# Re-dealing the rows of a block inverse, moving three small steps, and joining two matmuls in a hybrid decoder layer

## The chip, the cores and the metric

One core of a Trainium2 chip runs the whole layer. The time is the device time of that core in microseconds; lower is better. The kernel before has a median of 1421.55 us over three runs (1421.29 to 1422.97).

## What is computed

The layer takes 256 tokens of width 2048, puts 16 learned meta tokens ahead of them (272 in all), and computes:

- an embedding LayerNorm and one input projection `p = h @ w_in`;
- **an RWKV-7 mixer** of 16 heads of 64. Per token, with state S, `S = S*decay + (S @ -kk) (kk*a)^T + v k^T` and `y = S r`, where `kk` is the key scaled by `k_k` and divided by its norm over the head;
- a causal stick-breaking attention of 16 heads of 64, in 128-query blocks;
- a head norm of both, an output projection, `h = LN(alpha*h + mix)`;
- **a gated MLP**: `gate, val = split(h @ w_up)`, a causal width-3 convolution on gate, `(silu(gate)*val) @ w_down`, and a last LayerNorm. w_up has 2 x 5632 columns.

All data is float32.

## The kernel before

**Precision.** Every float32 operand x of a matmul is split in two fp32r parts, hi = round(x) and lo = x - hi, and a product is three matmuls: hi*hi, hi*lo, lo*hi (`passes`, lines 225 to 229). Weights arrive in 512 KB pieces on SP's queue; ScalarE makes hi (L183), VectorE makes lo (L186). `weight(i)` issues these some pieces ahead.

**Stages.** (1) 0 to 65 us: embedding norm, the first projections, and `lora()`, which makes decay and in-context rate (`sg`) of all eight head pairs by small matmuls, each evicted by a sigmoid on ScalarE. (2) 65 to 566 us: the mixers. (3) 566 to 700 us: the output projection's end and the first LayerNorm. (4) 700 to 1150 us: the up projection, tile by tile: tile 2f is gate, 2f+1 is val; a gate tile's matmuls have 258 moving columns, a val tile's 256, and each accumulates 16 k tiles x 3 matmuls in one PSUM bank. `act` (L1067) then does the convolution, silu, product, and split. Four of the banks rotate. (5) 1150 to 1405 us: the down projection, with 512 moving columns and, in its last fifth, partly 256.

**The order of the mixer stage.** PE's order is written out by hand. The input projection's matmuls run through `weave`, which counts them; after each 16 a `slot()` lets waiting tasks issue their own PE work. A task is a generator that yields (slots to wait, rank, PSUM banks needed of the two `misc` banks). The order of the other engines is left to a scheduler that goes by program order and readiness; weight casts are put 8 places later (`LATER`). Per head pair j there are:

- `rwkv_front(j)` (L558): a scan `cum` of the log decay, its exponentials `Pt` and `Pinv`, then `sq`, the squared scaled key, in hi and lo parts; two slots later PE sums it by head (tile `ss`, L536 and L537), and the normalised key and the products BK follow;
- `rwkv_back(j)` (L605): the products AG; two slots later PE makes the block products `gram` (L622), 18 pairs of 64x64; VectorE masks them (L624) and multiplies BK by PC (L626). GpSimd's queue carries the strictly lower 32x32 blocks through DRAM (`dl`) into LT. One slot later comes `bonus`, two slots later `bkt`, transposes of BK and v;
- for odd j `inverse(q)` (L664), q = j // 2: it inverts 36 blocks of 32x32 on GpSimd by 31 steps of a multiply and an add. Y holds 108 partitions = 3 groups (RG) of rows x 36 blocks, each partition 11 rows (NR) of 32. Row r lies in group r // 11, slot r % 11, and step s works on `min(s + 1, 11)` slots x 31 - s columns. Y goes through DRAM (`dy`) into TT by four DMAs on GpSimd's queue, one for each of four groups of 32 partitions;
- `chain(q)` (L683): 18 slots (INVERSE) after the two backs are done, nine chunks of three small products, the second of which (L705) reads TT. They end in `y` (L735), which takes both misc banks.

SP carries only weights and a few small loads; GpSimd's queue carries dl, LT, dy, TT and Y's start value.

Of the kernel before, what the change touches and what calls it, by code (L numbers as in the profile page):

```python
# [15 lines left out]
P = 128  # L16
# [63 lines left out]
def constants():  # L80
    c = np.zeros((P, NCV), np.float32)

    def put(name, a):
        o, w = CV[name]
        c[: a.shape[0], o:o + w] = a

    i = np.arange(P)
    put("ident", np.eye(P))
    put("bd", (i[:, None] // 64 == i[None] // 64) / 32)
    put("ones", np.ones((P, P)))  # L90
    put("tri", i[:, None] >= i[None])
    s, t, kind = i[:, None] % CH, i[None, :2 * CH] % CH, i[None, :2 * CH] // CH
    put("maskg", np.where(kind == 0, s < t, s <= t))
    put("cen", np.eye(P) - (i[:, None] // 64 == i[None] // 64) / 64)
    m = np.full((P, SBW), NEG, np.float32)
    for n, (k0, c0, c1, q0) in enumerate(ZB):
        key, q = k0 + i[:, None], q0 + np.arange(c1 - c0)[None]
        ok = key < q
        if n == 2:
            ok &= key >= 256  # L100
        m[:, c0:c1][ok] = 0
    put("sbmask", m)
    r = np.ones((P, TP))
    r[:, ::CH] = 0
    put("reset", r)
    y0 = np.zeros((RG, NB, NR, CH))
    for n in range(CH):
        y0[n // NR, :, n % NR, n] = 1
    put("y0", y0.reshape(RG * NB, NR * CH))
    return c  # L110

# [2 lines left out]
def hybrid_layer(ctx, tc, xin, cst, pvec, w2a2, g2, ln2, w_in, w_out, w_up, w_down, out, dbg=None):  # L114
# [169 lines left out]
    with ExitStack() as es:  # L284
# [106 lines left out]
        def lora():  # L391
            for m in range(3):
                shift(acc[m], 24 + m, lw[m], Q0 if m else 0)
            S.activation(lw[0][:64], lw[0][:64], AF.Tanh)
            sh = [tp_.tile([P, T], F32R, tag="tmp", bufs=2, name=f"sh{n}") for n in range(2)]
            for n, (h, o) in enumerate(zip(half, half[::-1])):
                S.copy(sh[n][h], lw[0][h])
                V.tensor_sub(sl[n][h], lw[0][h], sh[n][h].bitcast(F32))
                S.copy(sh[n][o], lw[0][h])
            yield  # L400
            for m in (1, 2):
                S.activation(lw[m][:, Q0:], lw[m][:, Q0:], AF.Sigmoid)
            S.copy(g1h, lw[1][:, Q0:])
            V.tensor_sub(g1l, lw[1][:, Q0:], g1h.bitcast(F32))
            S.copy(g2s[:96], lw[2][:96, Q0:])
            V.tensor_sub(g2s[32:64], lw[2][32:64, Q0:], g2s[32:64].bitcast(F32))
            for j in range(NPAIR):
                t = mtile(F32, f"sg{j}")
                G.memset(t[:, :, :PAD], 0.0)
                for n, name in enumerate(("w0", "a0")):  # L410
                    ps = pst.tile([P, 512], F32, tag="tr", bufs=4, name=f"lora{j}{n}")
                    w = w2a2_r[:, n, j * P:j * P + P]
                    mm(ps[:, :T], lhsT=w, rhs=sh[n], start=True, stop=False)
                    mm(ps[:, :T], lhsT=w, rhs=sl[n], start=False, stop=True)
# [142 lines left out]

    def rwkv_front(j, st):  # L558

        assert j == 0 or "bv" in state[j - 1]  # L560
        a = sg[j][:, 1]
        cum = atile("cum", [P, TP])
        V.tensor_tensor_scan(out=cum, data0=reset, data1=sg[j][:, 0], initial=0.0, op0=ALU.mult, op1=ALU.add)
        S.activation(Pt[:, :, 1:], ch(cum), AF.Exp, scale=-DECAY)
        Pinv = cum
        S.activation(Pinv, cum, AF.Exp, scale=DECAY)
        sq = atile("sq", [P, TP])
        S.activation(sq, k_, AF.Square, scale=par("k_k", j))
        sq = halves(sq, "rn", "ss")
        yield 2, FULL, 1  # L570
        ps = misc("ss")
        by_head(ps[:, :TP], *sq)
        ss = atile("ss", [P, TP])
        V.tensor_scalar(out=ss, in0=ps[:, :TP], scalar1=16.0, scalar2=0.5e-24, op0=ALU.mult, op1=ALU.max)
        rn = atile("rn", [P, TP])
        S.activation(rn, ss, AF.Ln, scale=2.0 * KSC)
        S.activation(rn, rn, AF.Exp, scale=-0.5, bias=lnb[:, 1:2])
        y2 = atile("sq", [P, TP])
        S.activation(y2, rn, AF.Square)
        V.tensor_mul(ss, ss, y2)  # L580
# [12 lines left out]
        st["kkn"] = kkn
# [11 lines left out]
    def rwkv_back(j, st):  # L605
# [8 lines left out]
        rk = halves(rk, "rkh", "rkl", NQ)  # L614
        PC = st["PC"] = atile("PC", [P, NCH], bufs=4)
        S.copy(PC, Pt[:, :, CH])
        yield 2, SQUARE, 2
        for c0, n in parts:
            ps = misc("gram").rearrange("p (c n) -> p c n", n=2 * CH)
            for c in range(n):  # L620
# [18 lines left out]
            bonus[j // 2] = wide(f"bv{j // 2}")  # L639
        bv = st["bv"] = bonus[j // 2][:, j % 2, :NQ]  # L640
        V.scalar_tensor_tensor(bv, ps[:, :NQ], 32.0, v_[:, TP - NQ:], op0=ALU.mult, op1=ALU.mult)
        yield 2, FULL, 2
        R = st["R"] = [wide(f"R{j}{x}").rearrange("p n t -> p (n t)").rearrange("p (c f) -> p c f", c=NCH) for x in range(2)]
        for x in range(2):
            V.memset(R[x], 0.0)
# [18 lines left out]
    def inverse(q, LT, Y):  # L664
# [1 line left out]
        tmp = atile("ytmp", [P, NR, CH])  # L666
        n_ = RG * NB
        for s in range(CH - 1):
            n = min(s + 1, NR)
            m = CH - 1 - s  # L670
            G.tensor_tensor(out=tmp[:n_, :n, :m], in0=Y[:n_, :n, s:s + 1].to_broadcast([n_, n, m]),  # L671
                            in1=LT[:n_, s:s + 1, s + 1:].to_broadcast([n_, n, m]), op=ALU.mult)
# [1 line left out]
        nc.gpsimd.dma_start(dy.rearrange("b (g r) t -> g b (r t)", g=RG), Y[:n_].rearrange("p r t -> p (r t)"))  # L674
        for n in range(4):
            x, o = n % 2, n * CH
            nc.gpsimd.dma_start(TT[q % 2][o:o + CH, :, CH - x * CH:2 * CH - x * CH],
                                dy[n * NCH:n * NCH + NCH, :CH].rearrange("c r t -> r c t"))

    def first_of_all():  # L680
        return tc.high_priority(offset=AHEAD)
# [255 lines left out]
    h1stack = ctx.enter_context(ExitStack())  # L937
    h1p = pool(h1stack, "h1p", side="right")

    h1hi = h1p.tile([P, KT, NQ + 2], F32R, name="h1hi")  # L940
    h1lo = h1p.tile([P, KT, NQ + 2], F32R, name="h1lo")
    for n, name in enumerate(("ln1_g", "ln1_b")):
        S.copy(h1hi[:, :, NQ + n], pars(name))
        V.tensor_sub(h1lo[:, :, NQ + n], pars(name), h1hi[:, :, NQ + n].bitcast(F32))
# [119 lines left out]
        S.copy(ahi[:, f], t)  # L1064
        V.tensor_sub(alo[:, f], t, ahi[:, f].bitcast(F32))

    def act(f, pg, pval):  # L1067
        t = up.tile([P, SEQ], F32, tag="t", bufs=2, name=f"t{f}")
        gate(f, t, pg, pval)
        split(f, t)  # L1070

# [46 lines left out]
    for f in range(4, NF):  # L1118
        pair = []
        for m in range(2):  # L1120
            ps = bank(f"u{2 * f + m}")
            n = NQ if m == 0 else SEQ
            for hf in range(2):
                hi, lo = weight(wi)
                wi += 1
                for kk in range(8):
                    kt = hf * 8 + kk
                    passes(ps[:, :n], hi, lo, kk, *rhs(m, kt), kt == 0, kt == KT - 1)
            pair.append(ps)
        act(f, *pair)  # L1130
    ustack.close()
    h1stack.close()

# [134 lines left out]
```

## Time and profile before

| | us |
|---|---|
| median of three runs | 1421.55 |
| the profiled execution | 1419.27 |
| its span, first to last instruction | 1417.5 |
| granted TensorE clock, mean (1 is 2.4 GHz) | 0.974 |

A group of instructions is given by source line, engine and tile; a wait by who waited for whom. PE is the matmul stream, PEld its weight loads, DVE VectorE, ACT ScalarE, POOL GpSimd. Matmuls overlap in the records, so a matmul's own duration is longer than the step from one to the next.

### The profile page before, as it was taken

How to read it: one execution, taken by the hardware profiler on the slowest of the kernel's cores; microseconds unless marked ns; L12 is line 12 of the kernel's file. 1: busy time of each engine (PE TensorE's matmuls, PEld its weight loads, DVE VectorE, ACT ScalarE, POOL GpSimd, SP SyncE). 2: the span in 40 equal slices, each digit the busy share in tenths (PEclk: the TensorE clock that was granted, in tenths of full speed). 3: DMA queues.
4: the chain of work that ended last, by engine and by line, in shares of the span. 5: the costliest groups of instructions: out<-in, count | busy, mean ns of one | idle time of the engine just before them, and what ended most of it. 6: DMA issues, size and time to landing. Idle time of an engine off the chain costs nothing.

```text
span 1417.5 us, 26265 instructions
## 1 busy us (share of the span) xinstructions
PE 1336.2 (94%) x10540; PEld 1250.2 (88%) x10540; DVE 937.4 (66%) x1502; ACT 723.3 (51%) x1227; POOL 278.1 (20%) x417
## 2 busy tenths in 40 slices
PE   8988798799999999988999999999999999999996
PEld 5888687788889889988999999999999998888895
DVE  7678666889876878888755555555555554445445
ACT  6755555566656766445644444444444443333331
POOL 4107873047282000553100000000000000000002
PEclk8999999999999999999999999999999999999998
DMA  7444433344444335543556665665666566656662
GB/s 228 136 126 144 127 114 91 95 126 120 136 120 116 110 93 165 160 151 112 162 193 194 185 185 179 183 187 181 180 186 185 180 222 210 192 184 190 201 183 89
DMA packets 67642, 224.02 MB, mean 158 GB/s; under 512 B 9144, under 2 KB 10868, under 8 KB 67376
## 3 DMA queue, kind: packets, MB, share of 16 engines
q1 hardware_dynamic: 63392, 215.03, 49.0%
q0 software_dynamic: 3264, 4.18, 1.3%
q10 hardware_dynamic: 864, 3.15, 0.6%
q8 instruction: 82, 1.34, 0.4%
q14 instruction: 40, 0.33, 0.1%
HBM read 219.01 MB, written 3.30 MB: 157 GB/s over the span
## 4 chain that ended last, share of the span: by engine, by line
PE 69%; DVE 8%; POOL 3%; ACT 3%; issue 2%; DMA 2%; POOLq 0%; DVEq 0%; ACTq 0%
PE u L229 11%; PE u L227 11%; PE u L228 11%; PE d L1148 6%; PE d L1147 6%; PE d L1149 6%; DVE wlo L186 2%; PE S L481 2%; PE S L483 2%; PE S L479 2%; POOL ytmp L671 1%; POOL Y L673 1%; PE R L479 1%; PE R L483 1%; PE R L481 1%
## 5 line engine op out<-in xcount | busy, mean ns | idle before, releaser
L186 DVE TENSOR_TENSOR wlo<-wraw,whi 128x1024 fp32r<-128x1024 f32 (+1 forms) x396 | 486.7, 1234 | 360.1 <-ACT whi L183 354.0
L183 ACT CAST whi<-wraw 128x1024 fp32r<-128x1024 f32 (+1 forms) x396 | 409.6, 1040 | 500.0 <-DMA wraw<-in_w_up_dram 104.2
L227 PE MATMUL u<-h1hi,whi 128*128 128x258 f32 (+2 forms) x1408 | 401.1, 285 | 2.3 <-ACT whi L183 2.3
L229 PE MATMUL u<-h1hi,wlo 128*128 128x258 f32 (+2 forms) x1408 | 398.6, 284 | 3.0 <-DVE wlo L186 3.0
L228 PE MATMUL u<-h1lo,whi 128*128 128x258 f32 (+2 forms) x1408 | 398.8, 284 | 0.0
L229 PEld LDWEIGHTS u<-h1hi,wlo 128*128 128x128 f32 x1408 | 268.1, 191 | 3.9 <-DVE wlo L186 3.9
L227 PEld LDWEIGHTS u<-h1hi,whi 128*128 128x128 f32 x1408 | 268.2, 191 | 3.2 <-ACT whi L183 3.0
L228 PEld LDWEIGHTS u<-h1lo,whi 128*128 128x128 f32 x1408 | 267.9, 190 | 0.1
L1148 PE MATMUL d<-wlo,ahi 128*128 128x512 f32 (+1 forms) x396 | 145.7, 368 | 0.0
L1147 PE MATMUL d<-whi,ahi 128*128 128x512 f32 (+1 forms) x396 | 145.6, 368 | 0.0
L1149 PE MATMUL d<-whi,alo 128*128 128x512 f32 (+1 forms) x396 | 145.3, 367 | 0.0
L1162 POOL TENSOR_TENSOR drs<-drs,mhalf 128x1 f32<-128x1 f32 x2 | 2.1, 1036 | 717.1 <-DVE drs L1161 717.1
L479 PE MATMUL S<-h,whi 128*128 128x272 f32 (+1 forms) x384 | 112.9, 294 | 1.7 <-DVE ql L806 1.7
L481 PE MATMUL S<-h,whi 128*128 128x272 f32 (+1 forms) x384 | 113.2, 295 | 0.0
L483 PE MATMUL S<-h,wlo 128*128 128x272 f32 (+1 forms) x384 | 113.0, 294 | 0.0
L479 PE MATMUL R<-h,whi 128*128 128x272 f32 (+1 forms) x352 | 104.5, 297 | 2.4 <-DVE shv L269 2.4
L483 PE MATMUL R<-h,wlo 128*128 128x272 f32 (+1 forms) x352 | 104.6, 297 | 0.0
L481 PE MATMUL R<-h,whi 128*128 128x272 f32 (+1 forms) x352 | 104.0, 296 | 0.0
L671 POOL TENSOR_TENSOR ytmp<-Y,LT 108x220 f32<-108x220 f32 (+29 forms) x124 | 82.1, 662 | 22.5 <-DMA LT<-dl 13.2
L1147 PEld LDWEIGHTS d<-whi,ahi 128*128 128x128 f32 x396 | 74.5, 188 | 13.2
L1149 PEld LDWEIGHTS d<-whi,alo 128*128 128x128 f32 x396 | 74.5, 188 | 13.0
L1148 PEld LDWEIGHTS d<-wlo,ahi 128*128 128x128 f32 x396 | 74.5, 188 | 12.7
(386 smaller groups left out, 2312.0 us busy)
## 6 DMA issues: line engine op xcount, KB each, us to landing
wraw<-in_w_up_dram SPq DMA_DIRECT2D x176, 512.0 KB, 3.5
wraw<-in_w_in_dram SPq DMA_DIRECT2D x96, 512.0 KB, 3.5
wraw<-in_w_down_dram SPq DMA_DIRECT2D x88, 512.0 KB, 4.2
wraw<-in_w_out_dram SPq DMA_DIRECT2D x28, 512.0 KB, 3.5
xraw<-in_w_in_dram SPq DMA_DIRECT2D x12, 256.0 KB, 3.8
xt<-in_xin_dram SPq DMA_DIRECT2D x8, 256.0 KB, 5.5
wraw<-in_w_out_dram SPq DMA_DIRECT2D x8, 256.0 KB, 2.6
l<-in_ln_dram ACTq DMA_DIRECT2D x1, 2048.0 KB, 8.1
```

The costliest lines, as they stand in the source:

```text
L183: S.copy(hi[:, :wide], raw[:, :wide])
L186: V.tensor_sub(lo[:, :wide], raw[:, :wide], hi[:, :wide].bitcast(F32))
L227: mm(ps, lhsT=hi[:, sl], rhs=xh, start=start, stop=False)
L228: mm(ps, lhsT=hi[:, sl], rhs=xl, start=False, stop=False)
L229: mm(ps, lhsT=lo[:, sl], rhs=xh, start=False, stop=stop)
L479: mm(ps, lhsT=hi[:, sl], rhs=xh, start=start, stop=False)
L481: mm(ps, lhsT=hi[:, sl], rhs=xl, start=False, stop=False)
L483: mm(ps, lhsT=lo[:, sl], rhs=xh, start=False, stop=stop)
L671: G.tensor_tensor(out=tmp[:n_, :n, :m], in0=Y[:n_, :n, s:s + 1].to_broadcast([n_, n, m]), in1=LT[:n_, s:s + 1, s + 1:].to_broadcast([n_, n ...
L1147: mm(ps, lhsT=ahi[:, f, t_], rhs=hi[:, w], start=f == 0, stop=False)
L1148: mm(ps, lhsT=ahi[:, f, t_], rhs=lo[:, w], start=False, stop=False)
L1149: mm(ps, lhsT=alo[:, f, t_], rhs=hi[:, w], start=False, stop=f == NF - 1)
```

## The change

Five edits:

1. Inverse: row r goes to group r % 3, slot r // 3, and step s works on s // 3 + 1 slots. Each of the four TT loads becomes three, one per group, which writes every third partition.
2. `rwkv_back`: gram waits three slots in place of two, bkt one after bonus in place of two.
3. `rwkv_front`: `sq` and its parts stand ahead of the scan and the exponentials.
4. `lora`: the gate's sigmoids and splits stand behind the eight pairs; four copies go from ScalarE to VectorE.
5. Up projection: h1hi and h1lo become one tile, and for val tiles (f from 4) hi x h1hi and hi x h1lo become one matmul of 512 moving columns, whose two halves `act` adds.

```diff
-        y0[n // NR, :, n % NR, n] = 1
+        y0[n % RG, :, n // RG, n] = 1
...
-                S.copy(sh[n][o], lw[0][h])
+                V.tensor_copy(sh[n][o], lw[0][h])
...
-            S.copy(g1h, lw[1][:, Q0:])
-            S.copy(g2s[:96], lw[2][:96, Q0:])
...
+            V.tensor_copy(g1h, lw[1][:, Q0:])
+            V.tensor_copy(g2s[:96], lw[2][:96, Q0:])
...
     def rwkv_front(j, st):
-        assert j == 0 or "bv" in state[j - 1]
         a = sg[j][:, 1]
+        sq = atile("sq", [P, TP])
+        S.activation(sq, k_, AF.Square, scale=par("k_k", j))
+        sq = halves(sq, "rn", "ss")
         cum = atile("cum", [P, TP])
...
-        sq = atile("sq", [P, TP])
-        S.activation(sq, k_, AF.Square, scale=par("k_k", j))
-        sq = halves(sq, "rn", "ss")
...
-        yield 2, SQUARE, 2
+        yield 3, SQUARE, 2
...
-        yield 2, FULL, 2
+        yield 1, FULL, 2
...
-            n = min(s + 1, NR)
+            n = s // RG + 1
...
-            nc.gpsimd.dma_start(TT[q % 2][o:o + CH, :, CH - x * CH:2 * CH - x * CH],
-                                dy[n * NCH:n * NCH + NCH, :CH].rearrange("c r t -> r c t"))
+            for g in range(RG):
+                k = len(range(g, CH, RG))
+                nc.gpsimd.dma_start(TT[q % 2][o + g:o + CH:RG, :, CH - x * CH:2 * CH - x * CH],
+                                    dy[n * NCH:n * NCH + NCH, g * NR:g * NR + k].rearrange("c r t -> r c t"))
...
-    h1hi = h1p.tile([P, KT, NQ + 2], F32R, name="h1hi")
-    h1lo = h1p.tile([P, KT, NQ + 2], F32R, name="h1lo")
+    h1 = h1p.tile([P, KT, 2, NQ + 2], F32R, name="h1")
+    h1hi, h1lo = h1[:, :, 0], h1[:, :, 1]
...
+        if parts > 1:
+            v = up.tile([P, SEQ], F32, tag="v", bufs=2, name=f"v{f}")
+            S.copy(v, pval[:, SEQ:])
+            V.tensor_add(v, v, pval[:, :SEQ])
+            pval = v
...
+                    if m == 0:
+                        passes(ps[:, :NQ], hi, lo, kk, *rhs(m, kt), kt == 0, kt == KT - 1)
+                        continue
+
+                    sl = slice(kk * P, kk * P + P)
+                    mm(ps, lhsT=hi[:, sl], rhs=h1[:, kt, :, 2:NQ], start=kt == 0, stop=False)
+                    mm(ps[:, :SEQ], lhsT=lo[:, sl], rhs=h1[:, kt, 0, 2:NQ], start=False, stop=kt == KT - 1)
```

## Rows read from the trace of the kernel before

**Rows 1.** Windows: busy us and count per engine, granted clock, DMA, two stages.

```profile
65.00:566.00 501.00, 453.21 (x4251) 420.69 (x4251) 395.83 (x805) 304.24 (x650) 193.15 (x312) 0.97 0.40 120
700.00:1150.00 450.00, 450.00 (x3744) 450.00 (x3743) 257.54 (x319) 208.76 (x279) 0.00 (x0) 1.00 0.60 185
```

**Rows 2.** Windows inside the up projection, the down projection, its last 256-column part.

```profile
725.00:1125.00 400.00, 400.00 (x3328) 400.00 (x3328) 226.95 (x279) 183.83 (x244) 0.00 (x0) 1.00 0.60 183
1175.00:1325.00 150.00, 150.00 (x655) 122.67 (x654) 71.33 (x64) 55.86 (x56) 0.00 (x0) 1.00 0.59 190
1396.20:1403.20 7.00, 7.00 (x61) 6.96 (x59) 6.84 (x11) 0.81 (x1) 3.69 (x5) 1.00 0.11 42
```

**Rows 3.** Waits of PE, 65 to 566 us: total us, times, longest.

```profile
PE chain L705 <- DMA TT<-dy: 12.5, 3, 7.0
PE ss L537 <- DVE ss L531: 4.2, 5, 1.3
PE gram L622 <- DVE AG L611: 4.1, 7, 1.7
PE ss L536 <- ACT rn L530: 3.9, 4, 1.9
...
PE R L479 <- DVE shv L269: 2.4, 1, 2.4
PE y L735 <- DVE BT L662: 2.3, 1, 2.3
PE gram L622 <- DVE BK L591: 2.2, 1, 2.2
...
PE gram L622 <- DVE gsq L544: 1.4, 1, 1.4
```

**Rows 4.** Windows in the mixer stage in which half the clock was granted.

```profile
78.20:85.00 6.80, 6.53 (x53) 6.41 (x54) 4.27 (x8) 1.24 (x2) 1.31 (x2) 0.50 0.35 90
...
170.40:180.40 10.00, 4.82 (x22) 4.33 (x24) 1.35 (x3) 1.45 (x3) 6.50 (x12) 0.50 0.36 108
231.80:238.50 6.70, 4.65 (x28) 4.24 (x29) 3.20 (x7) 1.33 (x4) 1.47 (x3) 0.50 0.24 66
276.20:282.80 6.60, 4.92 (x49) 4.89 (x50) 3.75 (x9) 2.70 (x7) 0.00 (x0) 0.50 0.01 2
```

**Rows 5.** POOL in order of time: start us, us; ends of inverses 0 and 1, their loads.

```profile
116.56 0.23 POOL L671 TENSOR_TENSOR ytmp<-Y,LT 108x31 f32<-108x31 f32 x1 [3.32 <-DMA LT<-dl]
...
166.18 0.23 POOL L673 TENSOR_TENSOR Y<-Y,ytmp 108x11 f32<-108x11 f32 x1
...
172.00 2.43 POOL L677 DMA_DIRECT2D TT<-dy  x4 [4.01 <-DMA dy<-Y]
...
183.01 0.23 POOL L671 TENSOR_TENSOR ytmp<-Y,LT 108x31 f32<-108x31 f32 x1 [2.32 <-DMA LT<-dl]
...
198.66 0.65 POOL L673 TENSOR_TENSOR Y<-Y,ytmp 108x220 f32<-108x220 f32 x1
...
223.96 0.48 POOL L673 TENSOR_TENSOR Y<-Y,ytmp 108x11 f32<-108x11 f32 x1
```

**Rows 6.** The tile TT, time of its loads to landing.

```profile
DMA to landing us min/median/max: 2.1/2.2/3.4
```

**Rows 7.** All engines in order of time: the key norm's parts of pair 2.

```profile
111.27 0.54 ACT L568 ACTIVATE sq<-shk,pv 128x288 f32<-128x288 f32 x1 [1.64 <-DVE shk L269]
...
111.72 1.03 ACT L183 CAST whi<-wraw 128x1024 fp32r<-128x1024 f32 x1
...
112.78 1.23 DVE L186 TENSOR_TENSOR wlo<-wraw,whi 128x1024 fp32r<-128x1024 f32 x1 [0.56 <-ACT whi L183]
```

**Rows 8.** In order of time: pair 3's gram, the last DVE step behind it, bkt.

```profile
154.08 0.29 PE L622 MATMUL gram<-AG,BK 64*64 64x64 f32 x2 [1.68 <-DVE AG L611]
...
158.79 0.74 DVE L626 TENSOR_TENSOR BK<-BK,PC 128x576 f32<-128x576 f32 x1
...
162.43 0.60 PE L649 MATMUL bkt<-cc,BK 128*128 128x128 f32 x4
```

More of the change, by code (lines that the diff above doesn't have):

```diff
@@ L398, in lora @@
                 V.tensor_sub(sl[n][h], lw[0][h], sh[n][h].bitcast(F32))
-                S.copy(sh[n][o], lw[0][h])
+                V.tensor_copy(sh[n][o], lw[0][h])
             yield
-            for m in (1, 2):
-                S.activation(lw[m][:, Q0:], lw[m][:, Q0:], AF.Sigmoid)
-            S.copy(g1h, lw[1][:, Q0:])
-            V.tensor_sub(g1l, lw[1][:, Q0:], g1h.bitcast(F32))
-            S.copy(g2s[:96], lw[2][:96, Q0:])
-            V.tensor_sub(g2s[32:64], lw[2][32:64, Q0:], g2s[32:64].bitcast(F32))
             for j in range(NPAIR):
@@ L417, in lora @@
                 yield
+            for m in (1, 2):
+                S.activation(lw[m][:, Q0:], lw[m][:, Q0:], AF.Sigmoid)
+            V.tensor_copy(g1h, lw[1][:, Q0:])
+            V.tensor_sub(g1l, lw[1][:, Q0:], g1h.bitcast(F32))
+            V.tensor_copy(g2s[:96], lw[2][:96, Q0:])
+            V.tensor_sub(g2s[32:64], lw[2][32:64, Q0:], g2s[32:64].bitcast(F32))
         order.enter_context(tc.manual_schedule(engines={PE.engine}))
@@ L1065, in split, with act @@
         V.tensor_sub(alo[:, f], t, ahi[:, f].bitcast(F32))
-    def act(f, pg, pval):
+    def act(f, pg, pval, parts=1):
         t = up.tile([P, SEQ], F32, tag="t", bufs=2, name=f"t{f}")
+        if parts > 1:
[3 more added lines that the diff above has]
+            pval = v
         gate(f, t, pg, pval)
@@ L1121, in hybrid_layer @@
             ps = bank(f"u{2 * f + m}")
-            n = NQ if m == 0 else SEQ
             for hf in range(2):
@@ L1127, in hybrid_layer @@
                     kt = hf * 8 + kk
-                    passes(ps[:, :n], hi, lo, kk, *rhs(m, kt), kt == 0, kt == KT - 1)
+                    if m == 0:
[4 more added lines that the diff above has]
+                    mm(ps[:, :SEQ], lhsT=lo[:, sl], rhs=h1[:, kt, 0, 2:NQ], start=False, stop=kt == KT - 1)
             pair.append(ps)
-        act(f, *pair)
+        act(f, *pair, 2)
     ustack.close()
```

## The prediction

> **What bounds the kernel now.** I read the windows by stage first. In the up projection PE and its weight loads are busy in every microsecond, at the full clock, while DVE and ACT are busy 57% and 46% of it and POOL not at all [rows 1]. This stage can get shorter only by what PE itself is given to do. In the mixer stage PE is busy 453 of 501 us, DVE 396 and ACT 304 [rows 1]: no engine is full there, so the stage is PE's work plus what PE waits for. The list of PE's waits says for what: 12.5 us for TT, three times, the longest 7.0; 7.7 for operands of gram (4.1, 2.2, 1.4); 8.1 for the two parts of the key norm (4.2 and 3.9) [rows 3]. The windows at half clock say what a wait costs besides: right behind the first gram, and around the TT waits of both groups, the granted clock is 0.50, that is 1.2 in place of 2.4 GHz, for 6.8, 10.0 and 6.7 us [rows 4]. Such a stretch costs half of the time in which PE works in it. A fourth, at 276 us beside y, I leave as it is.
>
> **The sum** is made against the profiled execution, 1419.3 us (span 1417.5), which lies 2.3 below the median of the runs, 1421.55. I carry the same saving over to the median. A measurement of this kernel can tell about 0.2%, 2.8 us, from no change.
>
> **Up projection.** For each val tile and k tile, three matmuls of 256 columns become one of 512 and one of 256. The columns stay 768; one instruction and one weight load go. A matmul of 256 or 258 columns starts every 400 / 3328 = 120.2 ns, one of 512 every 150 / 655 = 229.0 [rows 2]. Two of 256 take 240.4, so 11.4 ns go, 640 times (40 tiles x 16): **7.3 us, all on the path**, since PE is never idle there. Bounds: in the down projection's last part, 256 columns take 7.00 / 60 = 117 ns (60 being my estimate of the whole ones in that count) [rows 2], which leaves 5 ns or 3.2 us; a 512-column matmul without any overhead (213.3 at 2.4 GHz) would give 27 ns or 17 us. I take the first since it is the same stage. The two halves of the bank cost act a copy on ACT and an addition on DVE per tile; both engines have over 40% idle [rows 1] and a tile has 11.5 us until its banks are wanted again: nothing. The Trainium skill, page "TensorE: Matmul & The Clock Gate", section "Back-to-back issue gap", has a matmul at full clock start every N/2.4 + 2.5 ns. By that rule the pair would give back only 2.5 ns, 1.6 us in all, and the total would be 5.7 less; the rows do not agree with it (120.2 where it says 109.2, 229.0 where it says 215.8).
>
> **Gram a slot later.** A slot is 16 matmuls, 16 x 120 ns = 1.9 us [rows 2]. No wait for gram is longer than 2.2, so nearly all of the 7.7 us goes: **7.0** (between 0, if DVE only gets later by as much, and 7.7). With the first of them should go the half clock behind it, in which PE works 6.5 us: **3.3**. Against it, bkt keeps its slot, so it stands one slot nearer behind gram. For pair 3 gram starts at 154.1, DVE's last step before bkt ends at 159.5 and bkt starts at 162.4 [rows 8]; 2.9 of slack becomes 1.0. For some of the eight pairs DVE will be late, and y's wait for the banks behind bkt, 2.3 [rows 3], may grow: I put **1.0** against it (0 to 4).
>
> **Key norm's parts first.** In the order of time, sq starts as soon as the shifted key is there (111.27); what stands between it and PE is a weight cast (1.03) and a weight subtraction (1.23) [rows 7], not the scan and the exponentials, which were done before. Standing three places earlier, the parts may pass one of these now and then: **2.0** of the 8.1 (0 to 8.1).
>
> **Inverse.** Step s works on s//3 + 1 slots in place of min(s+1, 11). Summed over 31 steps, slots x columns fall from 3916 to 1991, in the multiply and in the add. Inverse 1 takes 183.0 to 224.4, 41.4 us; its shortest instruction, 0.23 us, times 62 is 14.3, which stays; 27.1 over 2 x 3916 elements is 3.5 ns each, and 3850 fewer elements give 13.3 us. An undisturbed instruction of 220 elements, 0.65, gives 2.0 ns per element and 7.7 us [rows 5]. I take **10 us per inverse** (7.7 to 13.3; inverse 0, 49.8 us long, has more in it). Against it: gram, and so the inverse, starts 1.9 us later; and twelve TT loads stand for four. Four take 2.43 us to issue, 0.61 each [rows 5], so the last is issued 8 x 0.61 = 4.9 later. For group 0 TT lands 10 - 1.9 - 4.9 = 3.2 us earlier, and of its 7.0 us wait 3.2 goes. Group 1's inverse is behind these loads on POOL's queue: it starts 3.2 earlier, is 10 shorter and has 4.9 more to issue, 8.3 in all; PE comes 3.2 earlier, so 5.1 of the other 5.5 us of wait goes. Together **8.0** (3 to 12.5). With group 1's wait the half clock beside it should go (PE works 4.7 us in it): **2.3**. Around group 0's remaining wait I leave the half clock as it is. And a loss: what PE gains between pair 1's gram and that first wait (pair 3's gram 1.7 [rows 8], some 1.0 of the key norm) only makes PE come earlier to the same TT: **2.7** back. Groups 2 and 3 do not wait for TT; the later loads have cover there.
>
> **Lora.** ACT loses four copies and DVE gains them, at a time at which ACT is fuller; but two sigmoids now stand behind the last pair, just ahead of the shift for which PE waits 2.4 us [rows 3]. I put **0.5** against it (-1.5 to 2).
>
> **What moves.** DVE is busy 79% of the mixer stage [rows 1] and has to do the same work in less time, so some waits will come back as waits for weight parts: **3.0** against the whole (0 to 10).
>
> Sum: 7.3 + 7.0 + 3.3 + 2.0 + 8.0 + 2.3 = 29.9; less 1.0 + 2.7 + 0.5 + 3.0 = 7.2; **22.7 us saved, 1396.6 for the profiled execution, 1398.9 for the median: 1399.**
>
> **Rival 1: the mixer stage gives nothing back.** DVE sets its pace, and each wait for gram, key norm or TT comes back as a wait for a weight part or a shift. For it: DVE's 79%, and the weight work that slips in between the parts [rows 7]. Against it: DVE has 105 us idle in that stage, and PE's waits for gram name DVE only because gram stands too early. Then only the up projection's 7.3 is left: 1414.3.
>
> **Rival 2: the twelve loads take more than the inverse gives (slower).** A load that writes every third partition may cost far more on POOL than the 0.61 us of one that writes 32 in a row; no row shows one. With p us each, group 0's TT comes 1.9 - 10 + (12p - 2.4) later and group 1's again -10 + (12p - 2.4). The rest of the change is worth some 17 us at that point (up projection 7.3, the first gram with its clock 5.5, gram and key norm behind group 1's first TT some 4, my estimate), so the kernel gets slower from p = 1.65. At p = 2.0 group 1's TT is 25.1 later, and the time 1421.6 + 25.1 - 16.8 = 1430. Against it: the loads land 2.2 us after issue in the median [rows 6] while the next one is issued after 0.61, so they overlap. The Trainium skill, page "DMA: Bandwidth & Descriptors", section "Anatomy of one DMA — SWDGE (gpsimd) path", gives each DMA issued from GpSimd a fixed cost of about 2.0 us. By that rule, taken one load after the other, this rival is what happens; as a latency it agrees with the 2.2 us of the trace.
>
> **How the numbers follow.** The forecast has 0.77. Its own range goes from 1386 (up projection 10, all waits for gram and TT gone, half of those for the key norm, nothing moved) to 1410 (DVE takes 10 back, each inverse gives 7.7). Rival 1 has 0.14, rival 2 has 0.05, and 0.04 is for something that I have not seen, on either side. The range that holds 8 in 10 takes in rival 1: 1385 to 1415. Faster by over 0.2% are the forecast, rival 1 and half of the rest: 0.92. Within 0.2% falls what is left of rival 1 with a small loss: 0.03. Slower: 0.05.
>
> **What would show it.** Up projection: a gate and a val tile take 48 x 120.2 + 16 x (229.0 + 120.2) ns = 11.36 us for 80 matmuls in place of 11.54 for 96, so 400 us hold about 2818. Inverse: its 62 instructions in 31 to 36 us, twelve TT loads of about 0.6 us, no PE wait for TT in group 1, about 4 to 6 us in group 0. Gram: waits below 1 us in all; the window behind the first gram at clock 1.00. Key norm: waits of 5 to 7 us still there. The forecast is wrong if the mixer stage is not 12 to 18 us shorter, or if waits for TT are as long as before.

## The result, and the profile after

| | before | after |
|---|---|---|
| median of nine runs each, us | 1421.55 | 1411.83 |
| ratio, with its 95% interval | | 0.9926 (0.9908 to 0.9944) |
| the profiled execution | 1419.27 | 1412.04 |
| its span | 1417.5 | 1410.3 |
| granted TensorE clock, mean | 0.974 | 0.971 |

The change saves 0.74%, 10.5 us by the ratio, where 22.7 were forecast. The windows by stage and the window inside the up projection, of the kernel after, in the columns of [rows 1] and [rows 2]:

```profile
65.00:566.00 501.00, 458.29 (x4244) 425.64 (x4242) 388.82 (x804) 301.55 (x649) 168.50 (x343) 0.95 0.39 120
700.00:1150.00 450.00, 450.00 (x3157) 421.12 (x3156) 270.30 (x361) 219.39 (x321) 0.00 (x0) 1.00 0.60 187
...
720.00:1120.00 400.00, 400.00 (x2803) 374.22 (x2802) 238.27 (x317) 192.79 (x281) 0.00 (x0) 1.00 0.59 186
```

In the same 501 us the mixer stage issues 4244 matmuls, with [rows 1] 4251: it is not faster at all. The mean clock of that stage falls from 0.97 to 0.95; added up over the trace, the stretches at half clock between 65 and 566 us grow from 34.1 to 47.8 us. From the first projection matmul of the stage to the first matmul of the output projection (tile o, at 516.3 us before) both kernels take 451.1 us; to the first matmul of tile o0b, at 563.4 us in both, it is 498.2 before and 499.7 after. What is saved shows in the up projection (from the first matmul of u to the first of d 527.1 before, 521.3 after), ahead of the stage (1.5), and behind the last matmul of d (2.1); 2.2 are lost between the first matmul of tile o and u. These are single executions, and they differ by some us where nothing was changed: b_val, one of the experiments below, has the mixer stage of before and takes 501.3 us to tile o0b, with 37.5 us of half clock.

So the question is where the mixer stage's share of the forecast, 15.4 us, went. The waits of PE between 60 and 566 us, after, in the columns of [rows 3]:

```profile
PE chain L706 <- DMA TT<-dy: 11.4, 4, 5.5
PE ss L536 <- ACT rn L530: 5.2, 4, 2.3
PE bonus L536 <- DVE AG L623: 4.4, 6, 1.5
PE ss L537 <- DVE ss L531: 2.7, 5, 0.8
...
PE vt L651 <- ACT BT L656: 2.0, 1, 2.0
...
PE gram L621 <- DVE psq L544: 1.1, 1, 1.1
...
PE gram L621 <- DVE AG L610: 0.5, 1, 0.5
```

The waits for gram's operands, 7.7 us in [rows 3], are 1.6. In their place stand bonus, which waits 4.4 for gram's masks (before, the line below), and vt, which waits 2.0 (not in the list before). TT has gone from 12.5 to 11.4 only.

```profile
PE bonus L536 <- DVE AG L624: 1.5, 3, 0.6
```

Yet the inverse did become as short as forecast. GpSimd in order of time, after: the ends of inverse 0 and inverse 1, their stores and their loads, against [rows 5]:

```profile
115.55 0.78 POOL L670 TENSOR_TENSOR ytmp<-Y,LT 108x31 f32<-108x31 f32 x1 [4.00 <-DMA LT<-dl]
...
153.61 0.23 POOL L672 TENSOR_TENSOR Y<-Y,ytmp 108x11 f32<-108x11 f32 x1
154.14 0.79 POOL L673 DMA_DIRECT2D dy<-Y  x1 [0.30 <-POOL Y L672]
...
159.97 6.98 POOL L678 DMA_DIRECT2D TT<-dy  x12 [4.40 <-DMA dy<-Y]
...
179.31 0.23 POOL L670 TENSOR_TENSOR ytmp<-Y,LT 108x31 f32<-108x31 f32 x1 [3.01 <-DMA LT<-dl]
...
210.64 0.23 POOL L672 TENSOR_TENSOR Y<-Y,ytmp 108x11 f32<-108x11 f32 x1
```

Inverse 0 takes 38.3 us (49.8 before), inverse 1 31.6 (41.4 before): 11.5 and 9.9 less. Twelve loads take 6.98 us to issue, 0.58 each. The first matmuls behind TT of groups 0 and 1, in order of time, before and then after:

```profile
174.93 0.44 PE L705 MATMUL chain<-Wt,TT 64*64 64x64 f32 x2 [7.00 <-DMA TT<-dy]
...
233.76 0.97 PE L705 MATMUL chain<-Wt,TT 64*64 64x64 f32 x4 [4.83 <-DMA TT<-dy]
```

```profile
166.88 0.44 PE L706 MATMUL chain<-Wt,TT 64*64 64x64 f32 x2 [5.46 <-DMA TT<-dy]
...
222.44 0.30 PE L706 MATMUL chain<-Wt,TT 64*64 64x64 f32 x2 [1.07 <-DMA TT<-dy]
226.52 0.44 PE L706 MATMUL chain<-Wt,TT 64*64 64x64 f32 x2 [3.78 <-DMA TT<-dy]
```

TT is there 8.1 us earlier for group 0 and 7.2 for group 1. The waits stay since PE arrives earlier by nearly as much (161.4 against 167.9 us for group 0): at both places TT still sets the time, and the time has moved. So at 226.5 us the kernel after is 7 us ahead. At 305 us it is not ahead any more: the 1153rd projection matmul starts at 305.3 in both. What lies between is pair 5, which takes 6 of the 7 us. Before, in order of time (PE, VectorE):

```profile
291.49 1.26 PE L622 MATMUL gram<-AG,BK 64*64 64x64 f32 x36
...
293.70 1.90 DVE L624 TENSOR_TENSOR AG<-gram,cc 64x320 f32<-64x320 f32 x4
...
294.96 0.28 PE L536 MATMUL bonus<-rkh,trbd 128*128 128x258 f32 x1
...
295.52 0.74 DVE L626 TENSOR_TENSOR BK<-BK,PC 128x576 f32<-128x576 f32 x1
...
295.74 0.36 PE L536 MATMUL gnv<-yh,trbd 128*128 128x258 f32 x1 [0.38 <-DVE AG L624]
```

And after:

```profile
285.41 0.28 PE L536 MATMUL gnv<-yh,trbd 128*128 128x258 f32 x1
...
288.10 0.43 DVE L544 SCALAR_TENSOR_TENSOR gsq<-gnv,gsq 128x258 f32<-128x258 f32 x1
288.11 1.09 PE L621 MATMUL gram<-AG,BK 64*64 64x64 f32 x30
288.56 0.43 DVE L545 SCALAR_TENSOR_TENSOR yh<-gsq,yh 128x258 f32<-128x258 f32 x1
289.02 0.43 DVE L771 TENSOR_TENSOR pt<-pt,yh 128x258 f32<-128x258 f32 x1
...
289.48 0.49 DVE L623 TENSOR_TENSOR AG<-gram,cc 64x320 f32<-64x320 f32 x1
290.01 1.23 DVE L186 TENSOR_TENSOR wlo<-wraw,whi 128x1024 fp32r<-128x1024 f32 x1
...
292.42 1.39 DVE L623 TENSOR_TENSOR AG<-gram,cc 64x320 f32<-64x320 f32 x3
293.05 0.36 PE L536 MATMUL bonus<-rkh,trbd 128*128 128x258 f32 x1 [1.48 <-DVE AG L623]
...
295.15 0.76 DVE L625 TENSOR_TENSOR BK<-BK,PC 128x576 f32<-128x576 f32 x1
...
299.78 0.43 DVE L640 SCALAR_TENSOR_TENSOR bv<-bonus,shv 128x258 f32<-128x258 f32 x1
300.06 0.53 PE L651 MATMUL vt<-cc,shv 128*96 128x128 f32 x3 [2.00 <-ACT BT L656]
```

Here is the main view. Before, gram is ahead of `gnv`, the sum by head of a pair that has been through its chain; its four masks run in one block of 1.90 us, and gnv comes behind them. A slot later, gram is **behind** gnv. What follows from gnv on VectorE (gsq, yh, pt) comes ahead of the masks, and a weight subtraction and four small steps of the gate and the chain come between them: they take from 289.48 to 293.81, 4.3 us. bonus waits 1.48 for them. bv, which reads bonus, runs 6.7 us behind it (before 1.2, at 296.18), and vt waits 2.00; there the profile names ScalarE's copies of bkt, which end at 300.01. So two things are late at this place: bonus behind the masks, and vt behind bkt, which stands one slot nearer; the experiments below take them apart. Around both waits the clock is down, in windows of the kernel after:

```profile
294.00:297.40 3.40, 3.40 (x16) 3.40 (x17) 3.27 (x8) 1.05 (x1) 1.49 (x4) 0.51 0.30 70
300.90:304.30 3.40, 3.40 (x19) 3.40 (x16) 0.66 (x3) 1.70 (x6) 2.31 (x10) 0.50 0.13 49
```

### The profile page after: what moved, and what is told of

Same layout as the page of the kernel before. It is cut to its first block, busy times and chain, and to the rows that moved or that the text cites. A ratio compares the mean times of both kernels' runs of the same rounds, so it can differ in the third digit from the quotient of the medians.

```text
span 1410.3 us, 25107 instructions
## 1 busy us (share of the span) xinstructions
PE 1336.0 (95%) x9900; PEld 1221.5 (87%) x9900; DVE 943.1 (67%) x1546; ACT 729.5 (52%) x1263; POOL 251.9 (18%) x449
## 4 chain that ended last, share of the span: by engine, by line
PE 68%; DVE 9%; issue 3%; POOL 3%; ACT 2%; DMA 2%; POOLq 0%; DVEq 0%; ACTq 0%
PE u L1138 11%; PE u L229 6%; PE u L227 6%; PE u L228 6%; PE d L1159 6%; PE d L1158 6%; PE d L1160 6%; PE u L1139 5%; DVE wlo L186 3%; PE S L481 2%; PE S L483 2%; PE S L479 2%; ACT whi L183 1%; POOL ytmp L670 1%; POOL Y L672 1%
## 5 line engine op out<-in xcount | busy, mean ns | idle before, releaser
L1138 PE MATMUL u<-h,whi 128*128 128x512 f32 x640 | 228.5, 398 | 0.0
L227 PE MATMUL u<-h,whi 128*128 128x258 f32 (+2 forms) x768 | 220.1, 287 | 1.9 <-ACT whi L183 1.9
L229 PE MATMUL u<-h,wlo 128*128 128x258 f32 (+2 forms) x768 | 217.9, 285 | 2.9 <-DVE wlo L186 2.9
L228 PE MATMUL u<-h,whi 128*128 128x258 f32 (+2 forms) x768 | 217.5, 284 | 0.0
L1139 PE MATMUL u<-h,wlo 128*128 128x256 f32 x640 | 180.1, 281 | 0.0
L229 PEld LDWEIGHTS u<-h,wlo 128*128 128x128 f32 x768 | 147.1, 192 | 4.0 <-DVE wlo L186 4.0
L227 PEld LDWEIGHTS u<-h,whi 128*128 128x128 f32 x768 | 146.4, 191 | 4.4 <-ACT whi L183 2.5
L228 PEld LDWEIGHTS u<-h,whi 128*128 128x128 f32 x768 | 147.1, 192 | 0.1
L1138 PEld LDWEIGHTS u<-h,whi 128*128 128x128 f32 x640 | 120.6, 189 | 27.6
L1139 PEld LDWEIGHTS u<-h,wlo 128*128 128x128 f32 x640 | 121.4, 190 | 0.0
L479 PE MATMUL S<-h,whi 128*128 128x272 f32 (+1 forms) x384 | 114.6, 298 | 1.6 <-DVE ql L807 1.6
L481 PE MATMUL S<-h,whi 128*128 128x272 f32 (+1 forms) x384 | 114.7, 299 | 0.0
L479 PE MATMUL R<-h,whi 128*128 128x272 f32 (+1 forms) x352 | 106.3, 302 | 2.4 <-DVE shv L269 2.4
L481 PE MATMUL R<-h,whi 128*128 128x272 f32 (+1 forms) x352 | 105.4, 300 | 0.0
```

What stands on the lines that cost most here:

```text
L227: mm(ps, lhsT=hi[:, sl], rhs=xh, start=start, stop=False)
L228: mm(ps, lhsT=hi[:, sl], rhs=xl, start=False, stop=False)
L229: mm(ps, lhsT=lo[:, sl], rhs=xh, start=False, stop=stop)
L479: mm(ps, lhsT=hi[:, sl], rhs=xh, start=start, stop=False)
L481: mm(ps, lhsT=hi[:, sl], rhs=xl, start=False, stop=False)
L1138: mm(ps, lhsT=hi[:, sl], rhs=h1[:, kt, :, 2:NQ], start=kt == 0, stop=False)
```

## The experiments

Eighteen kernels. Ratios are against runs of the kernel before on the same chip, and 0.001 is 1.4 us. First each part alone.

**Gram and bkt alone** (b_slots): the kernel before with

```diff
-        yield 2, SQUARE, 2
+        yield 3, SQUARE, 2
...
-        yield 2, FULL, 2
+        yield 1, FULL, 2
```

> The kernel before with the two yields alone (gram three slots, bkt one). Theory A, the wait is only moved: the masks on VectorE come no earlier, so what PE no longer waits for at gram it waits for at bonus and bkt; time within 3 us of before, PE's waits for gram, bonus and vt together 8 to 12 us as before (10.4). Rival B, the slot is worth what the prediction put on it: 8 to 10 us faster, those waits together below 4 us.

Ratio 1.0027 (1.0015 to 1.0038): 3.8 us slower. The waits of gram, bonus and vt come to 11.3 us (9.2 before), as theory A had it (its time, within 3 us of before, is just missed): they are moved and not gone. Waits of PE, 60 to 566 us:

```profile
PE chain L704 <- DMA TT<-dy: 15.2, 3, 9.7
PE bonus L536 <- DVE AG L623: 6.2, 6, 1.7
...
PE vt L651 <- ACT BT L656: 2.0, 1, 2.0
```

So the part forecast as the largest gain in the mixer stage is a loss.

**The inverse alone** (b_inv): the rows and the twelve loads.

```diff
-            n = min(s + 1, NR)
+            n = s // RG + 1
```

> The kernel before with the inverse and its twelve loads alone. Both theories: inverses of 30 to 38 us, TT waits of group 1 gone, of group 0 down to about 2 us. Theory A, gains in front of 280 us are given back behind it because VectorE is late there: 0 to 4 us faster. Rival B, they stay: 7 to 11 us faster.

Ratio 0.9939 (0.9925 to 0.9952): 8.7 us faster. PE's waits for TT are 9.4 us, the longest 4.3, so they did not go as expected. And not all of the 8.7 comes from TT. From the start of the last matmul of d to the end of the program it is 14.4 us in the traces of all ten kernels with the old inverse, and 12.2 to 12.3 in all ten with the new one. What is shorter there is the last long DRAIN instruction of GpSimd, at the program's end, 6.8 us before and 2.3 in b_inv (durations in ns, min/median/max; first b_inv, then before):

```profile
L1266 POOLq DRAIN  x3: 40/106/2319, 1407.4 to 1412.6; - x3
```

```profile
L1264 POOLq DRAIN  x3: 40/102/6811, 1409.9 to 1417.2; - x3
```

That is some 2.2 of the 8.7 us, in no term of the prediction. It is there with four loads too (a_ns_tt4), so it does not come from the twelve; why the drain is shorter is not shown.

**The joined matmuls alone** (b_val): tile h1, `act` and the loop over the tiles from f = 4.

```diff
-                    passes(ps[:, :n], hi, lo, kk, *rhs(m, kt), kt == 0, kt == KT - 1)
...
+                    mm(ps, lhsT=hi[:, sl], rhs=h1[:, kt, :, 2:NQ], start=kt == 0, stop=False)
+                    mm(ps[:, :SEQ], lhsT=lo[:, sl], rhs=h1[:, kt, 0, 2:NQ], start=False, stop=kt == KT - 1)
```

> The kernel before with the joined matmuls of the val tiles alone. The step that the profile after shows (512 columns 236 ns, the 256 behind it 118) gives 4 to 6 us; the step of the down projection, 229 ns, would give 7.3. Theory A has this as most of the whole gain; rival B as less than half of what the change could give.

Ratio 0.9969 (0.9958 to 0.9979): 4.4 us faster. The window inside its up projection has 2806 matmuls in 400 us, the kernel after 2803:

```profile
725.00:1125.00 400.00, 400.00 (x2806) 374.37 (x2805) 241.08 (x316) 195.45 (x281) 0.00 (x0) 1.00 0.59 186
```

**The key norm's order alone** (b_norm) and **lora alone** (b_lora):

```diff
+        sq = atile("sq", [P, TP])
+        S.activation(sq, k_, AF.Square, scale=par("k_k", j))
+        sq = halves(sq, "rn", "ss")
         cum = atile("cum", [P, TP])
...
-        sq = halves(sq, "rn", "ss")
```

> The kernel before with the key norm's parts ahead of the scan, alone. The parts start when the shifted key is there, whatever stands ahead in program order: PE's waits for them stay at 7 to 8 us and the time within 2 us of before. If the order were what held them: waits below 4 us, 3 to 6 us faster.

```diff
-            S.copy(g1h, lw[1][:, Q0:])
...
+            V.tensor_copy(g1h, lw[1][:, Q0:])
```

> The kernel before with the gate's sigmoids and splits behind the eight pairs and four copies on VectorE, alone. The first projection of the mixers starts 1 to 1.5 us earlier, as in the profile after (63.7 for 65.15), and the wait for the shift stays 2.4; 0 to 2 us faster.

0.9998 (0.9985 to 1.0011) and 0.9993 (0.9979 to 1.0006): neither can be told from nothing. The key norm's waits in b_norm are 4.2 and 4.1, as before. In b_lora the first projection matmul of the mixers starts at 65.0 us and not at 63.7; the kernels without lora's edit start it between 64.3 and 66.2, those with it between 63.7 and 65.8, so the 1.5 us saved ahead of the stage are not shown to be lora's. Together the five parts give 3.8 - 8.7 - 4.4 - 0.3 - 1.0 = -10.6, and the whole change 10.5: **the parts add up**, within intervals of 1.5 to 2 us on either side of each part; an effect between the parts of some 4 us could hide in that.

**All but the slots** (a_noslots): the kernel after with both yields at 2.

> The kernel after with the two yields set back to 2 and 2. Theory A: as fast as after or up to 4 us faster (1406 to 1413), waits for gram back at 6 to 8 us, for bonus below 2, TT lands 2 us earlier. Rival B: 7 to 10 us slower than after (1419 to 1422).

Ratio 0.9916 (0.9895 to 0.9938), 12 us faster than before; against the kernel after (0.9926) it cannot be told apart. bonus waits 0.9 us, and the list has no vt; gram's waits are back (2.9, 2.2, 1.4).

**Is it bkt, which stands nearer?** b_32 takes gram a slot later and leaves bkt's distance (3 and 2); b_21 leaves gram and takes bkt nearer (2 and 1).

```diff
-        yield 2, SQUARE, 2
+        yield 3, SQUARE, 2
```

> The kernel before with gram a slot later and bkt a slot later with it (yields 3 and 2), to hold against the run with yields 3 and 1 (ratio 1.0027). If the slot loses because bkt comes too near behind the masks: 3 to 6 us faster than that run, at or below before, no wait of vt. If it loses because gram's wait is only moved to bonus and TT comes later: within 2 us of that run, waits for bonus still 5 to 7 us, for TT 12 to 16.

```diff
-        yield 2, FULL, 2
+        yield 1, FULL, 2
```

> The kernel before with gram at its old place and bkt one slot after bonus in place of two: 3/1 lost 3.8 us and 3/2 lost 8.3. If the two shifts simply add, bkt a slot earlier is worth 4 to 5 us: 0.996 to 0.998. If they do not, 0.999 to 1.001; then 3/2's further loss is the chain that starts a slot later.

b_32: 1.0058 (1.0042 to 1.0073), 8.3 us slower; b_21: 1.0029 (1.0016 to 1.0043), 4.1 us slower. Neither came out as expected. Each alone loses at least as much as both together, so the shifts do not add in the whole time. That does not clear bkt's distance, since a bkt that is a slot later also puts the chain a slot later, and b_32 pays for that farther on; the table below and a_32 look at the place itself.

**Which pairs?** b_even and b_odd move gram for every other pair:

```diff
-        yield 2, SQUARE, 2
+        yield 3 - j % 2, SQUARE, 2
...
-        yield 2, FULL, 2
+        yield 1 + j % 2, FULL, 2
```

> The kernel before with the later gram for the even pairs alone, whose gram starts no inverse. If the loss of b_slots (ratio 1.0027) comes through the inverses (gram later, inverse later, TT later): nothing lost here, 0.997 to 1.000, with the first gram's 4 us kept until the first TT. If it comes from masks and bonus in every pair: 1.001 to 1.002.

(b_odd has `2 + j % 2` and `2 - j % 2`.)

> The same for the odd pairs alone. Through the inverses: the whole loss, 1.003 to 1.005, PE's waits for TT 2 to 4 us longer than the 12.5 of the kernel before. Masks and bonus in every pair: 1.001 to 1.002, TT as before.

b_even 0.9984 (0.9972 to 0.9996), b_odd 1.0062 (1.0041 to 1.0083): the odd pairs lose, as the theory of the inverses had it, and somewhat more. But the trace of b_odd puts most of it elsewhere:

```profile
PE chain L704 <- DMA TT<-dy: 16.6, 4, 11.2
...
PE bonus L536 <- DVE AG L623: 4.3, 6, 1.5
...
PE vt L651 <- ACT BT L656: 2.0, 1, 2.0
```

TT takes 4 us, most of which the first gram had given; 9 go between 261 and 316 us, 6 of them at pair 5 (table below). So two kernels leave out pair 5 alone:

```diff
-        yield 2, SQUARE, 2
+        yield 2 + (j != 5), SQUARE, 2
...
-        yield 2, FULL, 2
+        yield 1 + (j == 5), FULL, 2
```

> The kernel before with the later gram for all pairs but pair 5. If the loss is at that one place: two waits of 3.5 us and half of 6.8 us of half clock, some 7 us, come back, and 3.8 lost becomes 3 gained: 0.997 to 0.999. If every odd pair loses its share of the 8.8 (2.2 each): 1.001, or slower.

> The kernel after (0.9926 in nine runs) with pair 5 alone at its old slots. One place: 5 to 7 us faster than after, 0.987 to 0.989. Every odd pair: 2 us, 0.991.

b_no5: 1.0006 (0.9993 to 1.0020); a_no5: 0.9902 (0.9883 to 0.9920). Both are some 3 us better by the ratios than with pair 5 moved (the intervals overlap a little): about half of what was expected of this place, and it is not the only one. The time between fixed projection matmuls (their number in the stage) shows four places, us; where gram stands a slot later, bkt stands one nearer behind bonus:

| kernel, gram a slot later in | first gram (1 to 97) | first TT (577 to 673) | pair 5 (1057 to 1153) | pair 6 (1345 to 1441) |
|---|---|---|---|---|
| before, none | 19.6 | 26.4 | 19.0 | 18.6 |
| b_slots, all | 16.0 | 29.8 | 25.1 | 21.4 |
| b_even, even pairs | 14.5 | 27.1 | 19.0 | 20.9 |
| b_odd, odd pairs | 16.9 | 31.3 | 24.9 | 18.6 |
| b_no5, all but 5 | 14.5 | 29.8 | 19.1 | 22.5 |
| after, all | 14.5 | 26.1 | 25.1 | 21.3 |
| a_no5, all but 5 | 14.5 | 25.5 | 19.0 | 20.9 |
| a_noslots, none | 19.5 | 24.4 | 19.0 | 18.6 |

Four places. The first gram gains 3 to 5 us, as forecast (b_odd, in which pair 0 keeps its slots, gains 2.7 there too, so not all of it is gram's). At the first TT 1 to 5 go back wherever the odd pairs move. Pair 5 costs 6 us in each of these kernels that moves it and nothing in the others. Pair 6 costs 2 to 4 wherever the even pairs move, but most of that comes back: from 1345 to 1633 these kernels are 0.7 to 1.2 us behind (b_no5 3.7). Of pair 5's 6 us 1.2 come back in the next 96 matmuls. (These are single executions; the medians give pair 5's place 3 us in both comparisons.) In pair 6 PE's order has changed as in pair 5: before, gram stands ahead of `sbn`, the same sum for the attention (348.3 and 353.7 us), after, behind it (348.4 and 346.1). So it has in pair 4 (before, gram at 252.5 and sbn at 258.5; after, 248.1 and 244.9), where no loss shows: the 96 matmuls from 929 on take 30.2 us before, 30.1 in b_slots and 31.1 after.

**Are the broken masks the cause?** a_maskfirst is the kernel after with the masks and BK times PC put ahead of all other work of VectorE that is ready; a_ns_maskfirst is the same with both yields at 2.

```diff
-            for x, t in enumerate(toks):
-                V.tensor_mul(AG[x][t, c0:c0 + n], ps[t, :n], maskg[t].unsqueeze(1).to_broadcast([64, n, 2 * CH]))
...
+            with first_of_all():
+                for x, t in enumerate(toks):
+                    V.tensor_mul(AG[x][t, c0:c0 + n], ps[t, :n], maskg[t].unsqueeze(1).to_broadcast([64, n, 2 * CH]))
...
+        with first_of_all():
+            V.tensor_mul(BK, BK, PC.unsqueeze(2).to_broadcast([P, NCH, 2 * CH]))
```

> The kernel after with the four masks behind gram and the multiply of BK by PC ranked ahead of other work on VectorE. If the slot loses because other VectorE work is put between the masks (4.3 us for four where they took 1.9 back to back), this gives the slot back its worth: 5 to 9 us faster than after (1403 to 1407), waits for bonus and vt below 2 us. If the slot loses because bkt stands too near behind gram, whatever the masks do: within 2 us of after.

> The kernel after with the yields at 2 and 2 and the masks ranked first. The masks stood back to back there already, so the rank should change little: within 3 us of 1410. If the rank itself costs or gives (weights later, R later), it shows here: this is what the first run of this call is to be held against.

0.9905 (0.9890 to 0.9920) and 0.9874 (0.9854 to 0.9895). bonus's waits for the masks are gone in a_maskfirst, and it is 3 us below the kernel after by the ratios (the intervals overlap), where 5 to 9 were expected. Pair 5 still takes 25.1 us, as in the kernel after: vt still waits there (1.6), and the chain waits for VectorE's copies there (0.6 and 1.2). TT waits 13.4. a_ns_maskfirst is 4.4 faster than a_maskfirst (the intervals overlap a little) and 6.0 faster than a_noslots, where within 3 of it was expected: the ranks give something with the masks in one block too. So the masks in one block give nothing at pair 5, and the later gram costs beside them.

**bkt's old distance in the kernel after** (a_32: `yield 3`, `yield 2`):

> The kernel after with bkt two slots behind bonus again (yields 3 and 2), so that bkt and the chain come a slot later than in after. If bkt standing too near is what loses: 3 to 6 us faster than after. If the broken-up masks lose: within 2 us of after, waits for bonus still 3 to 5 us, those for vt gone.

0.9909 (0.9890 to 0.9927), the same as the kernel after. TT's waits fall to 8.7, but z waits 5.0 (a stick-breaking step) and gate 4.1, where the kernel after waits 0.6 and 1.2. Why these two come late I have not followed. The whole time hides what happens at pair 5: there a_32 takes 21.6 us and b_32 21.3, against 25.1 with bkt nearer and 19.0 with neither moved, and b_21, with bkt nearer alone, 22.4. So at this place some 2.5 of the 6 us are the later gram's and some 3.5 the nearer bkt's. Behind it the later bkt loses this again: from the 1153rd projection matmul to the last, a_32 takes 262.8 us and the kernel after 257.4, b_32 266.5 and b_slots 258.8. (Single executions again.)

**Four loads in place of twelve** (a_ns_tt4: a_noslots with the rows brought in order by the store):

```diff
-        nc.gpsimd.dma_start(dy.rearrange("b (g r) t -> g b (r t)", g=RG), Y[:n_].rearrange("p r t -> p (r t)"))
+        nc.gpsimd.dma_start(dy.rearrange("b (r g) t -> g b r t", g=RG), Y[:n_])
...
-            for g in range(RG):
...
+            nc.gpsimd.dma_start(TT[q % 2][o:o + CH, :, CH - x * CH:2 * CH - x * CH],
+                                dy[n * NCH:n * NCH + NCH, :CH].rearrange("c r t -> r c t"))
```

> The kernel after with the yields at 2 and 2 and the rows put back in order on their way out of Y (one store in pieces of 128 bytes), so that four TT loads do again. If the eight added loads cost what the prediction put on them (4.9 us per inverse), TT lands 4 to 5 us earlier, its waits fall from 8.9 to about 3 us and the time by 3 to 6 us against the kernel with the yields alone set back (1410): 1404 to 1407. If the store in small pieces takes as much as the loads give: same as that kernel.

A miss: 0.9921 (0.9901 to 0.9940), no better than a_noslots. GpSimd's idle time ahead of the TT loads, from the rows of tile TT, the kernel after and then a_ns_tt4:

```profile
  DMA dy<-Y: 15.3, 3
```

```profile
  DMA dy<-Y: 42.2, 4
```

The store, now in rows of 32 elements, lands later by more than the eight loads take to issue: from its issue to its landing it takes 11.6 to 15.6 us over the four inverses, in a_noslots 4.8 to 6.4, while the eight more loads of a_noslots take 4.6 to 5.9 us to issue.

**The version that beats both.** best19 is a_ns_maskfirst with the first two chains one slot later, since TT is still late there; best_p0 is best19 with the later gram for pair 0 alone, where the table shows a gain.

```diff
-        yield INVERSE, QUARTER_COLS, 0
+        yield INVERSE + (1 if q < 2 else 0), QUARTER_COLS, 0
```

> The kernel after with the yields at 2 and 2, the masks ranked first, and the chains of groups 0 and 1 one slot (1.9 us) later. The waits for TT, 7.8 us in the kernel without the last step, fall to 3 to 5; 1 to 4 us faster than that kernel (ratio 0.9874), so 0.985 to 0.987 of before. If what is gained there is only waited for behind it: the same ratio.

```diff
-        yield 2, SQUARE, 2
+        yield 3 if j == 0 else 2, SQUARE, 2
...
-        yield 2, FULL, 2
+        yield 1 if j == 0 else 2, FULL, 2
```

> The fastest version so far (gram at its old place, masks first, first two chains a slot later; ratio 0.9866) with the later gram for pair 0 alone. If the gain at the first gram is only given back at the first TT: 0.986 to 0.988. If it is kept: 4 us less, 0.983 to 0.985.

0.9866 (0.9838 to 0.9894) and 0.9849 (0.9829 to 0.9869), medians 1403.55 and 1401.99. Neither is clearly apart from a_ns_maskfirst (0.9874), but best_p0 is 11 us below the kernel after by the ratios. Its mixer stage, with 4339 matmuls in 501 us:

```profile
65.00:566.00 501.00, 463.77 (x4339) 432.44 (x4338) 397.71 (x820) 309.18 (x657) 177.60 (x349) 0.97 0.41 125
```

PE's list names no wait for TT any more, but the first product of group 0 that reads TT still waits 2.8 us, put down to "issue", and starts at 168.07, just after the last load of TT has landed (167.99): this wait is TT's too. bonus now waits 7.6 us for rkl, a step that the masks have been put ahead of.

## Why the prediction was wrong, step by step

It said 1399.0, faster. It is faster: 1411.8, with 10.5 us saved where 22.7 were forecast. It lies inside the range because the range took in rival 1. The prediction's own sign of being wrong came: the mixer stage is not 12 to 18 us shorter.

- **The step that failed is "Gram a slot later", 7.0 + 3.3 - 1.0 = 9.3 gained.** Alone it loses 3.8 (b_slots), 13.1 us short. The whole is 12.2 short (22.7 - 10.5); that this is so near is luck, since the other terms promised 4.6 too much and 5.6 too little. What the step said of the waits at gram came true: 7.7 became 1.6, and the first gram and its half clock gave 3.6 to 5.1 us. But **the waits moved and did not go**: those of gram, bonus and vt come to 9.2 us before, 11.3 in b_slots and 9.1 in the kernel after, and what the first gram gave went again at the first TT, which lands as late (group 0 at 175.9 us before, 175.6 in b_slots). The prediction named this as its lower bound (0, if DVE only gets later by as much) and put nearly all on the other end. It treated the eight pairs as alike and read them off pair 3, with nothing between gram, bonus and bkt. In pairs 0 to 3 nothing of a finished pair is about; in pairs 4 to 6 gram now stands behind an sbn or a gnv that it stood ahead of, and in pair 5 that place is dear. The trace of before shows how little room there is: from pair 5's gram (291.49) to its bonus (294.96) 3.5 us, in which 1.90 us of masks begin at 293.70; gnv alone brings three VectorE steps of 0.43 us ahead of them. I did not ask what gram is moved past, and the 1.0 for the nearer bkt was too small: at pair 5 alone it takes some 3.5 us. By the medians pair 5 is 3 of the 13.1 us; the rest is not traced to one place.
- **"TT: 8.0 + 2.3, less 2.7."** Measured alone 8.7 (b_inv), against the 8.0 + 2.3 that stand without the 2.7, which belongs to the gram step. It is less near than it looks: 2.2 of the 8.7 lie in the drain at the end, so that TT gave about 6.5 (my estimate, ratio less trace). 10 us per inverse came out as 9.9 to 11.9, and 0.61 per load as 0.58. The 1.9 us by which the later gram was to put off the inverse did not show: inverse 0 starts at 115.6 us in the kernel after and at 115.7 in a_noslots. The picture beside the sum was wrong: I expected no wait for TT in group 1 and half clock gone there; 4.8 us and 6.8 us of half clock stayed, because PE arrives nearly as much earlier as TT does. The half clock beside group 1's wait, kernel after:

```profile
225.80:232.60 6.80, 6.08 (x33) 5.79 (x34) 4.76 (x11) 1.33 (x4) 0.00 (x0) 0.50 0.23 71
```

- **Up projection, 7.3: the mechanism right, the size off; 4.4 alone.** 400 us hold 2803 matmuls, not 2818: 80 of them take 11.42 us, against 11.54 for 96 before, so 0.12 x 40 = 4.9 us. From start to start, a 512-column matmul takes 236 ns here (median), not the 229.0 of the down projection, and the 256 behind it 118. A rate of another stage was carried over, though the lower bound of 3.2 held. The Trainium skill, "TensorE: Matmul & The Clock Gate", section "Back-to-back issue gap", gives N/2.4 + 2.5 ns as the gap of an isolated matmul and says that a stream of weight loads and matmuls keeps another; the prediction took it for the stream. It would have given 1.6 us: too little, by this window as well.
- **Key norm, 2.0:** 0.3, not to be told from nothing, as the lower bound said. The reason given beside the term was the right one: what stands ahead of the parts are weight steps, and program order three places earlier does not pass them.
- **Lora, -0.5:** +1.0, not to be told from nothing, inside its bounds.
- **What moves, -3.0:** the single parts add up to the whole, within their intervals, so nothing of the kind is seen beside them; waits that come back elsewhere are real, but they lie inside the gram step.
- **Rival 1** (the mixer stage gives nothing back, 1414.3) is nearest in its number and in what the profile shows: 451.1 us to the first matmul of tile o, before and after. Its mechanism, VectorE as the pace of the whole stage, is not what happened: b_inv, whose changed work lies in that stage, is 8.7 us faster, 6.5 without the drain, and best_p0 takes 486.0 us to tile o0b where before takes 498.2, and issues 2% more matmuls in the same 501 us with VectorE busy for 398 us, nearly as before (396). One part gained and another lost.
- **Rival 2** (dear loads) fell: 0.58 us per load, and from issue to landing, kernel after:

```profile
DMA to landing us min/median/max: 1.9/2.9/4.7
```

The loads overlap. By the Trainium skill, "DMA: Bandwidth & Descriptors", section "Anatomy of one DMA — SWDGE (gpsimd) path", a fixed 2.0 us per DMA is near as a latency (1.9 at least and 2.9 in the median, here) and would be wrong as a cost of one after the other.

What stays open: the 2 to 4 us at pair 6 were not tested by a kernel of their own, only by the halves. Pair 5 was not tested with its gram later and its bkt at the old distance alone, so the split of its 6 us rests on kernels that move all pairs. The slots cost 3.8 us alone, but a_noslots is only 1.4 below the kernel after by the ratios, which the intervals do not tell from 0 nor from 3.8.

## What to carry to other kernels

When a step is moved in an order written by hand, list for every round of the loop what it now stands behind, and what that work puts on the engine that must answer it; one round read closely (here pair 3) says nothing of the rounds in which other tasks run. A wait that ends last can be moved by a slot and still be there: count the gain only if the engine waited for has its work done earlier, as with the inverse. And test each part alone: a change that gains 0.7% held one part that lost. Then look at the place itself and not at the whole time only: here the whole time of b_32 and a_32 hid that the nearer bkt is the larger part of the loss at pair 5.

## What the runs showed that I had not expected

Short waits are dear beyond their length: at pair 5 two waits, 1.48 and 2.00 us, come with two stretches of 3.4 us at a granted clock of 0.50, and the place costs 6.1 us in all. All waits of gram, bonus and vt between 60 and 566 us come to 9.2 us before and 9.1 after, while the half clock grows by 13.7 us. That where a wait falls counts beside how long it is may be read from this, but is not shown: between kernels with the same mixer stage (before and b_val) the half clock differs by 3.4 us, and b_inv, with its gram at the old place, has 41.8.

The new inverse also shortens the end of the program by 2.1 to 2.2 us, some 980 us after the last inverse: GpSimd's drain there takes 2.3 us in place of 6.8.
